# Hybrid encoder layer on one core: the order of four output products and the roles of two accumulator banks

## The chip, the cores and the metric

The kernel runs on one core of one Trainium2 chip. The metric is device time in microseconds (us): the median of three runs was 1156.17 us (1155.99 to 1157.1). Five engines work side by side, each through its own list of instructions in a fixed order: TensorE (PE, matmuls; its weight loads are listed as PEld), VectorE (DVE), ScalarE (ACT), GpSimd (POOL) and SyncE (SP, which here issues the DMAs). They wait for one another through semaphores only.

## The reference

One encoder layer over 4096 tokens of width 1024, in float32:

```
h    = rmsnorm(x) ;  proj = h @ w_in
q, k, v, g_a, u_p, g_p = split(proj)
a    = banded_attention(q, k, v, rel_bias, sink) * silu(g_a)    # 8 query heads, 2 kv heads, window 128
p    = multiscale_pool(u_p) * silu(g_p)                         # windows 2, 4, 8, 16
out  = x + rmsnorm(concat(a, p) @ w_out)
```

Banded attention takes blocks of 128 queries against three blocks of keys, adds a relative bias, appends a sink logit, and normalizes. The last line, the output projection `[a, p] @ w_out` with its norm, is the part whose order is changed.

## The kernel before

Every float32 operand of a matmul is kept as two float16 halves (high and low), so one product takes three matmuls for each slice of the contraction. The program has two halves. The first computes the gate and pooling projections and stores them; it isn't touched by the change. The second half walks over the sequence from its end to its start, in blocks of 128 queries (b = 31 down to 0) and in units of 256 tokens (unit u holds blocks 2u and 2u+1). For each unit it projects k, v and q, runs attention for both blocks, and multiplies the result by `w_out`.

That last multiplication is done with Strassen-Winograd sums: seven products of half size in place of eight. They are called 11, 12, 22, s1, s2, s3, s4 after the operand. Each is 12 matmuls of 128 x 512 (`product`, L1700, matmul L1708) into one PSUM bank. Two of them are added on top of another inside the bank (`acc=True`): 12 on 11, and s4 on s1. The left operands are made from the gated attention output and the pooled branch: ACT casts the high half to float16 (`high`, L1610), POOL subtracts to get the low half (`low`, L1614). Three sums on DVE (`sum1`, `sum3`, `sum2`, L1643 to L1649) and one on POOL (`sum4`) come ahead of the casts of s2, s3, s1 and s4.

What leaves the banks: `begin` (ACT copy, L1728) saves 11 by itself to `mo`, before 12 is added onto it in the same bank. `gain11` (DVE, L1738) and `square` (ACT, L1733) read 11+12 from that bank when it is complete. `add` (DVE, L1749) reads s2, s3, 22, s1 and s1+s4, each from its bank.

PSUM: three banks with the tags acc0, acc1 and acc2 are shared by all of the products, the projections of k, v and q (matmul L1300) and one side of the attention output (`values`, L1545). Four more banks hold scores (L1340), and one the other side of the output. A new use of a bank waits until all readers of the old one are done.

The order is written out by hand. `due(t, fn, ...)` puts a call with a planned time into a list; `pe(us, fn, ...)` does the same for TensorE and advances a planned clock `now`. At the end the list is sorted by planned time (and, where two are equal, by the order in which they were put in), and each engine gets its instructions in that order. An engine takes its instructions strictly in that order, whatever is ready. The steps of the loop (L2022) are, for odd b and u = b//2:

- scores of b, first half; s4 of unit u+2; k and v of unit u-1 into bank 2 (for b = 27 these two change places); `values` of b+1 into bank 0 (bank 1 for b = 27); scores of b, second half; then of unit u+1 the products 22 (bank 2), 11 (bank 0), s2 (bank 1), and 12 (bank 0, on 11).

and for even b:

- scores, first half; first half of q of unit u-1 into bank 1; `values` of b+1 into bank 0; scores, second half; second half of q into bank 1; then of unit u+1 the product s3 into bank 0 and s1 into bank 1.

A softmax (`softmax`, L1421) follows each scores: on DVE four `logits` (L1368), on ACT four `exps` (L1379), on DVE a reciprocal of the sums (`denominators`, L1386 and L1389), on ACT four `probs` (L1401), on DVE four `rests` (L1409), and a transposing DMA. `exps` also reads the sink logits, which POOL copies into the tile (`sinks`, L1351). The planned times that matter below, counted from T, the planned end of `values` in an odd step: cast of s2 T+1.8; the four `exps` T+1.9, T+2.7, T+3.5, T+4.3; `probs` from T+5.6; `rests` from T+6.2; casts of s3, s1 and s4 T+10.7, T+11.3, T+12.0, each with its `low` 0.65 later; the next `sinks` T+12.7. `begin` is planned for 1.0 before the end of product 11, `gain11` for the end of 12, `square` 0.1 after it, the `add` of s2 for the end of s2.

Thirty weight loads of one column (L1715; ten in the first units) are spread through each of 11, 22, s2 and 12; they run beside the matmuls.

Of the kernel before, what the change touches and what calls it, by code (L numbers as in the profile page):

```python
# [13 lines left out]
ALU = mybir.AluOpType  # L14
# [9 lines left out]
NB = S // P  # L24
# [15 lines left out]
O11, O12, O21, O22, OT1, OT2, OT4, OT3 = range(8)  # L40
HK = KT // 2
UT = 2 * P
NU = S // UT
# [95 lines left out]
def hybrid_layer(ctx: ExitStack, tc, io, out):  # L139
    nc = tc.nc  # L140
# [74 lines left out]
    with ExitStack() as actx:  # L215
# [23 lines left out]
        def turn(name):  # L239
            turns[name] += 1  # L240
            return turns[name] % 2
# [386 lines left out]
        def pair(q, op, i, scale, key, group):  # L628
            src, r, w = raws[q][:, i], quarter_keys(q, i), f"w{slot[q, op]}"
            do("ACT", act(D) + 0.1, key, w_high, q, op, src, scale, r=r + [f"sw{group}"],  # L630
               w=[f"{w}h"])
            do("DVE", dve(D) + 0.06, key + 0.1, w_low, q, op, src, scale,
               r=r + [f"sw{group}", f"{w}h"], w=[f"{w}l"])
# [343 lines left out]
        b = turn("n2")  # L977
        for j in range(4):
            ld(9.5 + 0.1 * j, wut[:, j], io["w_uT"][j], 0.5, w=[f"wut{j}"])
            z = turn("sq")  # L980
            for half in range(2):
                t = U0 + 4 * j + 2 * half
# [291 lines left out]
    gpost = pb1.tile([P, D], F32, name="gpost")  # L1274
# [41 lines left out]
    def due(t, fn, *args):  # L1316
        plan.append((t, len(plan), fn, args))
# [103 lines left out]
    def softmax(b, half, t):  # L1421

        for i in range(4):
            due(t + 0.1 + 0.67 * i, logits, b, half, i)
            due(t + 0.8 + 0.8 * i, exps, b, half, i)
            due(t + 4.5 + 0.6 * i, probs, b, half, i)
            due(t + 5.1 + 0.62 * i, rests, b, half, i)
        due(t + 4.3, denominators, b, half)
        due(t + 7.8, turn, b, half)
# [159 lines left out]
    at, yf, y_t, mo_t, z_t, ss_t, xr_t, rs_t = {}, {}, {}, {}, {}, {}, {}, {}  # L1589
# [74 lines left out]
    LO, HI = slice(0, 512), slice(512, D)  # L1664
    last_z = {}

    def last_product(i, name, o, c, first):

        if first:

            n = {(1, 0): 0, (1, 1): 2, (0, 0): 1}.get((i, c))
            last_z[i, c] = (
                gemm.tile([P, 512], F32, name=f"z{i}{c}", tag=f"acc{n}") if n is not None
                else s_t[0][:, 0]
            )
        y = y_t[0, name]
        n = 0
        for k in range(HK):
            for yi, wi in ((0, 0), (0, 1), (1, 0)):
                nc.tensor.matmul(  # L1680
                    last_z[i, c], y[:, k, yi, :], wo[o][:, wi, k, :],
                    start=(first and n == 0), stop=(not first and n == 3 * HK - 1),
                    skip_group_check=True,
                )
                n += 1
# [31 lines left out]
    def open_unit(u):  # L1717
        if u > 1:
            mo_t[u] = [
                pb.tile([P, D], F32, name=f"mo{u}_{i}", tag=f"mo{i}", bufs=2 - i) for i in range(2)  # L1720
            ]
        else:
            mo_t[u] = [spare32("x", 2 * u + i) for i in range(2)]
        ss_t[u] = pb.tile([P, 4], F32, name=f"ss{u}", tag="ss")

    def begin(u):
        open_unit(u)
        nc.scalar.copy(mo_t[u][0][:, HI], z_t[u, 0])  # L1728

    def square(u, i, c, bank=None):  # L1730
        junk = pb.tile([P, 512], BF16, name=f"jkb{u}_{i}{c}", tag="junk", bufs=1)
# [2 lines left out]
            junk, src, AF.Square, scale=2.0**-5, accum_out=ss_t[u][:, 2 * i + c : 2 * i + c + 1]  # L1734
        )

    def gain11(u):
        nc.vector.tensor_tensor(  # L1738
            out=mo_t[u][0][:, LO], in0=z_t[u, 0], in1=gpost[:, LO], op=ALU.mult
        )  # L1740

    def gain(u, i, cs, eng=nc.gpsimd):
# [47 lines left out]
    def pe(us, fn, *args):  # L1790

        due(now[0], fn, *args)
        now[0] += us
        return now[0]
# [4 lines left out]
    def visit(b, half):  # L1799
        now[0] = max(now[0], free[0])  # L1800
        t = max(pe(1.1, scores, b, half), free[1])
        softmax(b, half, t)
        free[:] = t + 2.9, t + 7.9
# [10 lines left out]
    def do_q(u, half, late=0.0, bank=1):  # L1814
        due(pe(5.3, proj_q, u, half, bank) - 1.0 + late, keep_q, u, half)

    def attend(b, bank):
        t = pe(2.0, values, b, bank)
        due(t - 0.3, copy_o, b)
        due(t, gate, b)  # L1820
        if b % 2:
            pair(t + 0.8, b // 2, "11", a11)
        else:
            sums(b // 2, t + 0.7)

    M = 2.6
    SP0 = 10

    def spaces(u):
        return 30 if u < NU - 2 else SP0  # L1830

    def mix_p1(u):
        due(pe(M, product, u, "11", O11, 0, None, spaces(u)) - 1.0, begin, u)

    def mix_p4(u):
        pe(M, product, u, "22", OT4, 2, None, spaces(u))

    def mix_p2(u):
        t = pe(M, product, u, "12", O21, 0, True, spaces(u))
        due(t, gain11, u)  # L1840
        due(t + 0.1, square, u, 0, 0, 0)

    def mix_p6(u):
        due(pe(M, product, u, "s2", OT2, 1, None, spaces(u)), add, u, (0, HI), (0, HI), 1)

    def mix_p7(u):
        t = pe(M, product, u, "s3", OT3, 0)
        due(t - 2.0, add, u, (1, HI), (0, HI), 0)
        due(t - 1.9, add, u, (1, LO), (1, HI), 2)
        due(t + 1.4, square, u, 1, 0)  # L1850
        due(t + 2.0, gain, u, 1, LO)

    def mix_p5(u):
        t = pe(M, product, u, "s1", OT1, 1)
        due(t, add, u, (1, HI), (1, HI), 1)
        due(t + 0.7, square, u, 1, 1)
        due(t + 1.4, gain, u, 1, HI)
        finish(u, 1, t + 4.0)

    def mix_p3(u):  # L1860
        bank = int(u < NU - 1)
        t = pe(M, product, u, "s4", O22, bank, True)
        due(t, add, u, (0, HI), (0, HI), bank)
        due(t + 0.7, square, u, 0, 1)
        due(t + 1.4, gain, u, 0, HI)
        due(t + (5.5 if u == NU - 1 else 4.0), mean, u, 0)
        due(t + 13.1, residual, u, 0, slice(0, D))
        due(t + 14.5, store, u, 0, slice(0, D))
# [11 lines left out]
    def at_(t, fn, *args):  # L1880
        due(z + t, fn, *args)
# [140 lines left out]
    for b in reversed(range(2, NB - 4)):  # L2022
        u = b // 2
        t0 = now[0]
        due(t0 + 10.0, load_ga, b)
        if b % 2 == 0 and b > 2:
            due(t0 + 9.0, load_xr, u + 1, 1)
            due(t0 + 9.0, load_xr, u + 1, 0)
        visit(b, 0)
        if b % 2:  # L2030
            for step in ((do_kv, u - 1), (mix_p3, u + 2))[:: 1 if b == NB - 5 else -1]:
                step[0](step[1])
            attend(b + 1, int(b == NB - 5))
            visit(b, 1)
            mix_p4(u + 1)
            mix_p1(u + 1)
            mix_p6(u + 1)
            mix_p2(u + 1)
        else:
            do_q(u - 1, 0)  # L2040
            attend(b + 1, 0)
            visit(b, 1)
            do_q(u - 1, 1)
            due(now[0] + 2.1, load_x, u - 3)
            if b > 2:
                mix_p7(u + 1)
                mix_p5(u + 1)
        if b % 2:
            due(now[0] - 1.0, pool_in, u, 0)
            due(now[0] + 2.0, pool_in, u, 1)  # L2050
            pair(t0 + 8.1, u + 1, "22", a22)
            pair(t0 + 8.7, u + 1, "12", a12)
# [3 lines left out]
    z = now[0]  # L2056

    at_(0.0, scores, 1, 0)
    at_(1.1, product, 2, "s3", OT3, 0)
    at_(3.7, product, 2, "s1", OT1, 1)  # L2060
    at_(6.3, product, 1, "11", O11, 0)
    at_(8.9, product, 2, "s4", O22, 1, True)
    at_(11.5, values, 2, 2)
    at_(13.6, scores, 1, 1)
    at_(14.7, product, 1, "12", O21, 0, True)
    at_(17.3, product, 1, "22", OT4, 2)
    at_(19.9, scores, 0, 0)
    at_(20.8, product, 1, "s2", OT2, 1)
    at_(23.4, product, 1, "s3", OT3, 0)
    at_(26.0, product, 1, "s1", OT1, 1)  # L2070
    at_(28.6, scores, 0, 1)
    at_(29.5, last_product, 1, "22", O21, 0, True)
    at_(32.1, product, 1, "s4", O22, 1, True)
    at_(34.7, values, 1, None)
    at_(36.8, last_product, 1, "22", O22, 1, True)
    at_(39.4, last_product, 0, "12", O21, 0, True)
# [9 lines left out]
    soft(0, 0, 24.9, 25.6, 29.4, 29.5, 29.7, 31.7)  # L2086
    soft(0, 1, 31.6, 32.3, 34.3, 34.4, 34.5, 36.5)

    at_(3.7, add, 2, (1, HI), (0, HI), 0)
    at_(5.5, add, 2, (1, LO), (1, HI), 2)  # L2090
    at_(6.2, add, 2, (1, HI), (1, HI), 1)
    at_(7.0, square, 2, 1, 0)
    at_(9.9, square, 2, 1, 1)
    at_(11.5, add, 2, (0, HI), (0, HI), 1)
    at_(12.3, square, 2, 0, 1)
    at_(11.1, gain, 2, 1, LO, V)
    at_(11.8, gain, 2, 1, HI, V)
# [3 lines left out]

    cast(5.8, 6.4, 1, "22", a22, G)
    cast(6.4, 10.2, 1, "12", a12, G)
    at_(9.0, begin, 1)
    at_(13.7, gate, 2)
    at_(14.4, sum1, 1)
    at_(15.1, sum3, 1)
# [1 line left out]
    at_(16.55, sum4, 1)  # L2109
    cast(16.6, 18.9, 1, "s2", a11, V)  # L2110
    cast(20.5, 20.55, 1, "s3", a21, G)
    at_(19.1, gain11, 1)
    at_(16.58, square, 1, 0, 0, 0)
    cast(21.7, 21.8, 1, "s1", a_s1, G)
    at_(22.3, add, 1, (0, HI), (0, HI), 1)
    cast(24.8, 25.0, 1, "s4", a12, G)
    at_(27.0, add, 1, (1, HI), (0, HI), 0)
    at_(27.7, add, 1, (1, LO), (1, HI), 2)
    at_(28.5, square, 1, 1, 0)
    at_(28.6, add, 1, (1, HI), (1, HI), 1)  # L2120
    at_(31.2, square, 1, 1, 1)
    at_(35.0, add, 1, (0, HI), (0, HI), 1)
    at_(36.6, square, 1, 0, 1)
    at_(40.7, gain, 1, 1, LO, V)
    at_(41.4, gain, 1, 1, HI, V)
# [110 lines left out]
```

## Time and profile before

| | before |
|---|---|
| median of 3 runs | 1156.17 us (1155.99 to 1157.1) |
| the profiled execution's own time | 1156.7 us |
| its span, first to last instruction | 1154.8 us |
| PE busy | 1141.8 us, 99% of the span |
| DVE busy | 941.0 us, 81% |
| ACT busy | 717.3 us, 62% |
| POOL busy | 313.5 us, 27% |
| granted TensorE clock, mean | 0.995 |

A busy PE isn't a PE at its peak, since the ends of matmuls are modelled; the starts are recorded. In lists of instructions over time, the columns are: start in us from the start of the span, duration in us, engine, line, operation, output<-inputs, shape, and how many were merged into the row (x12); in brackets the idle time of the engine just before it, with what ended it. In groups by wait, the columns are total us, times and the longest.

### The profile page before, as it was taken

How to read it: one execution, taken by the hardware profiler on the slowest of the kernel's cores; microseconds unless marked ns; L12 is line 12 of the kernel's file. 1: busy time of each engine (PE TensorE's matmuls, PEld its weight loads, DVE VectorE, ACT ScalarE, POOL GpSimd, SP SyncE). 2: the span in 40 equal slices, each digit the busy share in tenths (PEclk: the TensorE clock that was granted, in tenths of full speed). 3: DMA queues.
4: the chain of work that ended last, by engine and by line, in shares of the span. 5: the costliest groups of instructions: out<-in, count | busy, mean ns of one | idle time of the engine just before them, and what ended most of it. 6: DMA issues, size and time to landing. Idle time of an engine off the chain costs nothing. (4 is left out here: it accounts for less than half of the span.)

```text
span 1154.8 us, 37344 instructions
## 1 busy us (share of the span) xinstructions
PE 1141.8 (99%) x15196; PEld 898.3 (78%) x16676; DVE 941.0 (81%) x1874; ACT 717.3 (62%) x1485; POOL 313.5 (27%) x309
## 2 busy tenths in 40 slices
PE   8999999999999999999999999999999999999997
PEld 6998888888888888886667677677776767767743
DVE  7989969987898973468788887878888888787886
ACT  7875545646565442266666776676667667667672
POOL 0102121111111110210434433532533443343231
PEclk8999999999999999999999999999999999999999
DMA  9644677776567565299976887787888698778795
GB/s 341 232 138 123 247 230 247 247 260 225 188 207 254 174 165 153 65 279 242 262 179 149 198 216 135 208 197 174 182 200 191 147 198 214 134 205 162 139 253 158
DMA packets 301701, 228.66 MB, mean 198 GB/s; under 512 B 219568, under 2 KB 259504, under 8 KB 296928
## 3 DMA queue, kind: packets, MB, share of 16 engines
q1 hardware_dynamic: 301536, 226.30, 73.9%
q8 instruction: 124, 2.03, 0.7%
q14 instruction: 41, 0.34, 0.1%
HBM read 114.68 MB, written 60.34 MB: 152 GB/s over the span
## 5 line engine op out<-in xcount | busy, mean ns | idle before, releaser
L703 PEld LDWEIGHTS <-wq 128*128 128x128 f16 x4104 | 402.0, 98 | 46.6
L703 PE MATMUL y<-xt,wq 128*128 128x256 f16 x1512 | 175.8, 273 | 0.0
L1300 PE MATMUL aq<-xb,xb 128*128 128x256 f16 x1024 | 173.4, 273 | 0.2 <-DVE q L1290 0.2
L1379 ACT ACTIVATE p<-p,nm 128x385 f32<-128x385 f32 (+1 forms) x256 | 152.8, 598 | 30.5 <-POOL p L1351 19.1
L1300 PEld LDWEIGHTS <-xb 128*128 128x128 f16 x1536 | 150.2, 98 | 26.5 <-issue 8.2
L1708 PE MATMUL ms<-wo,ys 128*128 128x512 f16 x720 | 164.4, 379 | 0.5 <-DVE mo L1749 0.5
L1409 DVE SCALAR_TENSOR_TENSOR pn<-p,rd,pn 128x384 f16<-128x384 f32 (+1 forms) x256 | 154.9, 657 | 6.3 <-ACT pn L1401 6.2
L1368 DVE CUSTOM_DVE_ANT_0 p<-s,nt,nsink 128x384 f32<-128x384 f32 (+1 forms) x256 | 155.9, 665 | 1.7 <-PE s L1340 1.7
L1300 PE MATMUL aq<-xb,xt 128*128 128x256 f16 x512 | 139.6, 273 | 0.0
L1401 ACT ACTIVATE pn<-p,rd 128x384 f16<-128x384 f32 (+1 forms) x256 | 135.0, 596 | 5.6 <-ACT p L1379 2.2
L311 POOL TENSOR_TENSOR yt<-yt,sg 128x512 f32<-128x512 f32 (+2 forms) x32 | 51.1, 1596 | 321.4 <-DVE yt L314 252.3
L1708 PE MATMUL m<-wo,y 128*128 128x512 f16 x540 | 121.8, 379 | 0.0
L1708 PEld LDWEIGHTS <-ys 128*128 128x128 f16 x720 | 68.7, 97 | 66.8 <-issue 3.8
L1300 PE MATMUL kv<-xb,xb 128*128 128x256 f16 x512 | 86.8, 273 | 0.0
L1744 POOL TENSOR_TENSOR mo<-mo,gpost 128x512 f32<-128x512 f32 x39 | 63.8, 1635 | 82.9 <-ACT jkb L1733 81.8
L1300 PEld LDWEIGHTS <-xt 128*128 128x128 f16 x768 | 75.1, 98 | 9.8 <-issue 0.2
L1715 PEld LDWEIGHTS <-y 128*1 128x1 f16 x1110 | 44.9, 83 | 35.4
L1300 PE MATMUL kv<-xb,xt 128*128 128x256 f16 x256 | 69.8, 273 | 0.0
L813 ACT COPY cc<-y 128x512 f32<-128x512 f32 x42 | 24.5, 584 | 69.5 <-PE y L703 57.4
L703 PE MATMUL plain<-xb,wq 128*128 128x256 f16 x576 | 67.3, 276 | 0.0
L1386 DVE TENSOR_SCALAR den<-den 128x4 f32<-128x4 f32 x64 | 11.8, 184 | 64.2 <-ACT p L1379 64.2
L1614 POOL TENSOR_TENSOR ys<-at,ys 128x512 f16<-128x512 f32 x28 | 37.4, 1334 | 89.1 <-ACT ys L1610 54.8
(223 smaller groups left out, 2008.7 us busy)
## 6 DMA issues: line engine op xcount, KB each, us to landing
nt<-in_xT SPq DMA_DIRECT2D x28, 512.0 KB
x_scr<-xb SPq DMA_DIRECT2D x14, 1024.0 KB
xb<-x_scr SPq DMA_DIRECT2D x14, 1024.0 KB
xr<-in_x SPq DMA_DIRECT2D x28, 512.0 KB
out<-xr SPq DMA_DIRECT2D x28, 512.0 KB
xn<-in_x SPq DMA_DIRECT2D x27, 512.0 KB
ga_scr<-cc SPq DMA_DIRECT2D x64, 128.0 KB
raw<-in_w_out SPq DMA_DIRECT2D x16, 512.0 KB
```

The source lines that it names most:

```text
L311: eng.tensor_tensor(out=out, in0=in0, in1=in1, op=op)
L703: nc.tensor.matmul(b[:, s], wq[:, slot[q, op], wv, s, k, :], x[:, xv, k, :], start=(first and k + s + wv + xv == 0), stop=(last and k == H ...
L813: A.copy(dst, bank_t[bk])
L1300: nc.tensor.matmul(acc, w[:, j, k, :], x[:, kh, v, kt, :], start=(n == 0), stop=(n == 3 * KT - 1),)
L1368: nc.vector.tensor_tensor_reduce(out=p_t[b, half][:, hh, :nk], in0=s_t[jj][:, gg, :nk], in1=bias[:, h, lo : lo + nk], scale=negc[:, h : h ...
L1379: nc.scalar.activation(p[:, hh, : nk + 1], p[:, hh, : nk + 1], AF.Exp, bias=nm_t[b, half][:, hh : hh + 1], scale=-1.0, accum_out=den_t[b, ...
L1401: nc.scalar.activation(prob_view(b, half)[:, 0, i], p_t[b, half][:, i, :nk], AF.Copy, scale=rd_t[b, half][:, i : i + 1],)
L1409: nc.vector.scalar_tensor_tensor(out=pn4[:, 1, i], in0=p_t[b, half][:, i, :nk], scalar=rd_t[b, half][:, i : i + 1], in1=pn4[:, 0, i], op0= ...
L1614: eng.tensor_tensor(out=y[:, :, 1], in0=f(u), in1=y[:, :, 0], op=ALU.subtract)
L1708: nc.tensor.matmul(z_t[u, tag], y[:, k, yi, :], wo[o][:, wi, k, :], start=(n == 0 and acc is None), stop=(n == 3 * HK - 1), skip_group_che ...
L1715: nc.tensor.ldweights(y[:, k, yi, :1])
L1744: eng.tensor_tensor(out=mo, in0=mo, in1=gpost[:, cs], op=ALU.mult)
```

## The change

In the loop, the four products of an odd step come in the order 11, 22, 12, s2 instead of 22, 11, s2, 12. Banks 0 and 1 change roles in what follows, in the loop and in the written-out end: `values` goes to bank 1, both halves of q to bank 0, s3 to bank 1, s1 and s4 to bank 0. 11 and 12 stay in bank 0 and s2 in bank 1 in the loop; in the written-out end for units 2, 1 and 0 all of bank 0 and bank 1 are exchanged. No instruction is added or removed, and no operand's size is changed. The planned times are computed from the order, so `begin`, `gain11`, `square` and the `add` of s2 get other planned times too.

```diff
@@ last_product
-            n = {(1, 0): 0, (1, 1): 2, (0, 0): 1}.get((i, c))
+            n = {(1, 0): 1, (1, 1): 2, (0, 0): 0}.get((i, c))
@@
-    def begin(u):
+    def begin(u, bank=0):
         open_unit(u)
-        nc.scalar.copy(mo_t[u][0][:, HI], z_t[u, 0])
+        nc.scalar.copy(mo_t[u][0][:, HI], z_t[u, bank])
@@
-    def gain11(u):
+    def gain11(u, bank=0):
         nc.vector.tensor_tensor(
-            out=mo_t[u][0][:, LO], in0=z_t[u, 0], in1=gpost[:, LO], op=ALU.mult
+            out=mo_t[u][0][:, LO], in0=z_t[u, bank], in1=gpost[:, LO], op=ALU.mult
         )
@@
     def mix_p7(u):
-        t = pe(M, product, u, "s3", OT3, 0)
-        due(t - 2.0, add, u, (1, HI), (0, HI), 0)
+        t = pe(M, product, u, "s3", OT3, 1)
+        due(t - 2.0, add, u, (1, HI), (0, HI), 1)
...
     def mix_p5(u):
-        t = pe(M, product, u, "s1", OT1, 1)
-        due(t, add, u, (1, HI), (1, HI), 1)
+        t = pe(M, product, u, "s1", OT1, 0)
+        due(t, add, u, (1, HI), (1, HI), 0)
...
     def mix_p3(u):
-        bank = int(u < NU - 1)
-        t = pe(M, product, u, "s4", O22, bank, True)
-        due(t, add, u, (0, HI), (0, HI), bank)
+        t = pe(M, product, u, "s4", O22, 0, True)
+        due(t, add, u, (0, HI), (0, HI), 0)
@@ the loop
-            attend(b + 1, int(b == NB - 5))
+            attend(b + 1, 1)
             visit(b, 1)
+            mix_p1(u + 1)
             mix_p4(u + 1)
-            mix_p1(u + 1)
+            mix_p2(u + 1)
             mix_p6(u + 1)
-            mix_p2(u + 1)
         else:
-            do_q(u - 1, 0)
-            attend(b + 1, 0)
+            do_q(u - 1, 0, bank=0)
+            attend(b + 1, 1)
             visit(b, 1)
-            do_q(u - 1, 1)
+            do_q(u - 1, 1, bank=0)
@@ the written-out end: 0 and 1 exchanged in every product, add, begin, gain11 and square
-    at_(6.3, product, 1, "11", O11, 0)
+    at_(6.3, product, 1, "11", O11, 1)
...
-    at_(9.0, begin, 1)
+    at_(9.0, begin, 1, 1)
...
```

In the loop, `mix_p1` is product 11, `mix_p4` 22, `mix_p2` 12 and `mix_p6` s2.

More of the change, by code (lines that the diff above doesn't have):

```diff
@@ L2058, in hybrid_layer @@
     at_(0.0, scores, 1, 0)
-    at_(1.1, product, 2, "s3", OT3, 0)
-    at_(3.7, product, 2, "s1", OT1, 1)
-    at_(6.3, product, 1, "11", O11, 0)
-    at_(8.9, product, 2, "s4", O22, 1, True)
+    at_(1.1, product, 2, "s3", OT3, 1)
+    at_(3.7, product, 2, "s1", OT1, 0)
+    at_(6.3, product, 1, "11", O11, 1)
+    at_(8.9, product, 2, "s4", O22, 0, True)
     at_(11.5, values, 2, 2)
     at_(13.6, scores, 1, 1)
-    at_(14.7, product, 1, "12", O21, 0, True)
+    at_(14.7, product, 1, "12", O21, 1, True)
     at_(17.3, product, 1, "22", OT4, 2)
     at_(19.9, scores, 0, 0)
-    at_(20.8, product, 1, "s2", OT2, 1)
-    at_(23.4, product, 1, "s3", OT3, 0)
-    at_(26.0, product, 1, "s1", OT1, 1)
+    at_(20.8, product, 1, "s2", OT2, 0)
+    at_(23.4, product, 1, "s3", OT3, 1)
+    at_(26.0, product, 1, "s1", OT1, 0)
     at_(28.6, scores, 0, 1)
     at_(29.5, last_product, 1, "22", O21, 0, True)
-    at_(32.1, product, 1, "s4", O22, 1, True)
+    at_(32.1, product, 1, "s4", O22, 0, True)
     at_(34.7, values, 1, None)
@@ L2087, in hybrid_layer @@
     soft(0, 1, 31.6, 32.3, 34.3, 34.4, 34.5, 36.5)
-    at_(3.7, add, 2, (1, HI), (0, HI), 0)
+    at_(3.7, add, 2, (1, HI), (0, HI), 1)
     at_(5.5, add, 2, (1, LO), (1, HI), 2)
-    at_(6.2, add, 2, (1, HI), (1, HI), 1)
+    at_(6.2, add, 2, (1, HI), (1, HI), 0)
     at_(7.0, square, 2, 1, 0)
     at_(9.9, square, 2, 1, 1)
-    at_(11.5, add, 2, (0, HI), (0, HI), 1)
+    at_(11.5, add, 2, (0, HI), (0, HI), 0)
     at_(12.3, square, 2, 0, 1)
@@ L2111, in hybrid_layer @@
     cast(20.5, 20.55, 1, "s3", a21, G)
-    at_(19.1, gain11, 1)
-    at_(16.58, square, 1, 0, 0, 0)
+    at_(19.1, gain11, 1, 1)
+    at_(16.58, square, 1, 0, 0, 1)
     cast(21.7, 21.8, 1, "s1", a_s1, G)
-    at_(22.3, add, 1, (0, HI), (0, HI), 1)
+    at_(22.3, add, 1, (0, HI), (0, HI), 0)
     cast(24.8, 25.0, 1, "s4", a12, G)
-    at_(27.0, add, 1, (1, HI), (0, HI), 0)
+    at_(27.0, add, 1, (1, HI), (0, HI), 1)
     at_(27.7, add, 1, (1, LO), (1, HI), 2)
     at_(28.5, square, 1, 1, 0)
-    at_(28.6, add, 1, (1, HI), (1, HI), 1)
+    at_(28.6, add, 1, (1, HI), (1, HI), 0)
     at_(31.2, square, 1, 1, 1)
-    at_(35.0, add, 1, (0, HI), (0, HI), 1)
+    at_(35.0, add, 1, (0, HI), (0, HI), 0)
     at_(36.6, square, 1, 0, 1)
```

## The prediction

> **What bounds the kernel now.** I read the page first, then the PE's rows of one unit in the second half, then the other engines' rows of the same stretch, and last the groups of waits.
>
> ```profile
> span 1154.8 us, 37344 instructions
> ...
> PE 1141.8 (99%) x15196; PEld 898.3 (78%) x16676; DVE 941.0 (81%) x1874; ACT 717.3 (62%) x1485; POOL 313.5 (27%) x309
> ...
> PEclk8999999999999999999999999999999999999999
> ```
>
> PE is busy for 99% of the span at a full clock, so a change moves the time only by making PE stop, or by taking away a stop that it has. The PE rows of the unit with its second scores at 860.17:
>
> ```profile
> 850.55 0.60 PE L1708 MATMUL ms<-wo,ys 128*128 128x512 f16 x2
> ...
> 860.17 0.96 PE L1340 MATMUL s<-k_all,q 64*32 64x288 f16 x48
> 861.06 5.35 PE L1708 MATMUL m<-wo,y 128*128 128x512 f16 x24
> 866.25 2.88 PE L1708 MATMUL ms<-wo,ys 128*128 128x512 f16 x12
> 868.97 0.38 PE L1708 MATMUL m<-wo,y 128*128 128x512 f16 x1
> ...
> 871.65 0.93 PE L1340 MATMUL s<-k_all,q 64*32 64x288 f16 x48
> 872.51 0.28 PE L1300 MATMUL aq<-xb,xb 128*128 128x256 f16 x1
> ...
> 891.82 0.60 PE L1708 MATMUL ms<-wo,ys 128*128 128x512 f16 x2
> ```
>
> They are s4, scores, 22 and 11 together, s2, the start of 12, the next scores, the first q, and s4 of the next unit. One unit takes 891.82 - 850.55 = 41.27 us, with nothing between the products: 22 and 11 take 5.19, or 2.60 each. Only s2 is longer, 868.97 - 866.25 = 2.72, and a group of the waits says why; the row under it is the view of `begin`'s line:
>
> ```profile
> PEld L1708 <- POOL ys L1614: 2.7, 12, 0.2
> ```
>
> ```profile
> L1728 ACT COPY mo<-m x14: 560/564/586, 531.7 to 1074.3; 128x512 f32<-128x512 f32 x14
> ```
>
> In 12 units the third matmul of s2 waits for POOL's low half; the cost to PE is 2.72 - 2.60 = 0.12. `begin` counts the units: the first two of the 14 are 15 (written out) and 14; the other 12, units 13 to 2, follow each other at 41.27.
>
> ACT in the same stretch (s2 cast, three of four `exps`, `begin`, first `probs`, casts of s3 and s1, `square`, cast of s4, next `exps`), then DVE (reciprocal of the sums, residual, `rests`, `add` of s2, `gain11`) and POOL (low half of s2, s3, s1, s4, and `sinks`):
>
> ```profile
> 864.88 0.62 ACT L1610 CAST ys<-at 128x512 f16<-128x512 f32 x1 [3.75 <-DVE at L1649]
> 865.54 0.62 ACT L1379 ACTIVATE p<-p,nm 128x385 f32<-128x385 f32 x1
> ...
> 866.16 0.60 ACT L1379 ACTIVATE p<-p,nm 128x385 f32<-128x385 f32 x1
> ...
> 866.76 0.60 ACT L1379 ACTIVATE p<-p,nm 128x385 f32<-128x385 f32 x1
> ...
> 867.95 0.56 ACT L1728 COPY mo<-m 128x512 f32<-128x512 f32 x1
> 868.55 2.13 ACT L1401 ACTIVATE pn<-p,rd 128x384 f16<-128x384 f32 x4
> 870.59 0.60 ACT L1610 CAST ys<-at 128x512 f16<-128x512 f32 x1
> 871.85 0.62 ACT L1610 CAST ys<-s 128x512 f16<-128x512 f32 x1 [0.66 <-PE m L1708]
> 873.04 0.60 ACT L1733 ACTIVATE jkb<-m 128x512 bf16<-128x512 f32 x1 [0.57 <-DVE mo L1738]
> 873.53 0.19 ACT L1733 ACTIVATION_READ_ACCUMULATOR jkb<-m 128x1 f32 x1
> 873.62 0.61 ACT L1610 CAST ys<-yf 128x512 f16<-128x512 f32 x1
> 875.63 0.62 ACT L1379 ACTIVATE p<-p,nm 128x385 f32<-128x385 f32 x1 [1.40 <-POOL p L1351]
> ```
>
> ```profile
> 868.08 0.17 DVE L1386 TENSOR_SCALAR den<-den 128x4 f32<-128x4 f32 x1 [0.83 <-ACT p L1379]
> ...
> 868.40 1.28 DVE L1771 SCALAR_TENSOR_TENSOR xr<-mo,rs,xr 128x1024 f32<-128x1024 f32 x1
> 869.61 2.20 DVE L1409 SCALAR_TENSOR_TENSOR pn<-p,rd,pn 128x384 f16<-128x384 f32 x4
> 871.72 0.68 DVE L1749 TENSOR_TENSOR mo<-ms,mo 128x512 f32<-128x512 f32 x1
> 872.32 0.68 DVE L1738 TENSOR_TENSOR mo<-m,gpost 128x512 f32<-128x512 f32 x1
> ```
>
> ```profile
> 865.58 1.16 POOL L1614 TENSOR_TENSOR ys<-at,ys 128x512 f16<-128x512 f32 x1 [2.86 <-PE m L1708]
> ...
> 871.26 1.57 POOL L1614 TENSOR_TENSOR ys<-at,ys 128x512 f16<-128x512 f32 x1 [3.29 <-ACT ys L1610]
> 872.79 1.16 POOL L1614 TENSOR_TENSOR ys<-s,ys 128x512 f16<-128x512 f32 x1
> 874.31 1.16 POOL L1614 TENSOR_TENSOR ys<-yf,ys 128x512 f16<-128x512 f32 x1 [0.36 <-ACT ys L1610]
> 875.41 0.32 POOL L1351 COPY p<-nsink 128x4 f32<-128x4 f32 x2
> ```
>
> Two rows matter most. `square` waited 0.57 for `gain11`, though it uses nothing that `gain11` makes: both read the bank of 11+12, and the second reader waits for the first. And the next `exps` (875.63) had waited 1.40 for `sinks`, which stand on POOL behind the three low halves.
>
> **The change part by part.** Times are on the clock of this unit, with 860.17 held fixed.
>
> (a) s2 goes last. Its low half ends at 866.74, s2 then starts after 12; the stop of 0.12 goes, in 12 units.
>
> (b) `begin`. Planned for T+5.3 before, it is now planned for T+1.1+2.6-1.0 = T+2.7. That is behind the cast of s2 (T+1.8) and the first `exps`, and level with the second `exps` (T+2.7 too). Adding the plan's numbers in floating point, the tie falls `begin` ahead of the second `exps` in units 13, 12 and 11 and behind it in 14 and 10 to 2. ACT waits for DVE's sums until 864.88, so `begin` starts at 866.76 (866.16 in the three) and takes 0.56. 12 must wait for it. Without a wait 12 would start at 866.25, the old place of s2. With the 0.07 from ACT's end to PE's start (as between ACT's cast, 870.59 + 0.60, and POOL's start, 871.26) it starts at 867.39 or 866.79, 1.14 or 0.54 late. Before, `begin` had ended at 868.51 and 12 started at 868.97: a cover of 0.46, gone.
>
> (c) Behind `begin` on ACT stand `exps` 3 and 4 (in the three units also 2), 0.59 later each (867.95 to 868.55). DVE's reciprocal, the residual and `rests` are a chain without gaps behind them, so DVE comes free at 871.72 + 0.59 = 872.31.
>
> (d) `gain11` and `square` move up, since 12 ends earlier. `gain11` takes DVE's slot at 872.31, ends at 873.00; `square` starts at 873.03. But on ACT `square` (T+9.0) now stands ahead of the casts of s3, s1 and s4 (T+10.7 on), and holds them up while it waits. The cast of s3 goes from 870.59 to 873.03 + 0.59 = 873.62.
>
> (e) The banks. The first q now takes bank 0, after `gain11` and `square`, where it took bank 1 after the `add` of s2. `square`'s sum is out 0.69 after its start (873.04 to 873.53 + 0.19), so with 0.06 to PE's start q begins at about 873.78, not 872.51: 1.27 late, in all units, whether (b) costs 0.54 or 1.14. All other exchanges put a use behind one as old as before: 0 and 1 are swapped in both. 22 and 11 find their banks free for longer.
>
> (f) POOL. The low half of s3 starts 0.69 after its cast (as 873.62 to 874.31 for s4), at 874.31, and s1 and s4 follow at 1.10 each (874.31 to 875.41). For s3 I take 1.16, not 1.57, since it no longer runs beside `add` and `gain11`. So `sinks` starts at 874.31 + 3.30 = 877.61 and the `exps` 0.22 later, at 877.83, not 875.63: 2.20 late.
>
> (g) From these `exps` a chain runs over ACT and DVE through the first q's low half, `rests`, the gate, the next softmax and the three `add`s to s4 of the unit. How long it is when nothing else holds it up is seen in unit 14, where PE did wait for it:
>
> ```profile
> 587.11 0.62 ACT L1379 ACTIVATE p<-p,nm 128x385 f32<-128x385 f32 x1 [1.41 <-POOL p L1351]
> 602.91 0.59 PE L1708 MATMUL ms<-wo,ys 128*128 128x512 f16 x2 [0.47 <-DVE mo L1749]
> ```
>
> 15.80 us. In the steady unit it is 891.82 - 875.63 = 16.19, so the chain has 0.39 to spare. Late by 2.20, it brings s4 at 877.83 + 15.80 = 893.63, 1.81 late. PE's stops at 12, at q and at s4 are not added: each is counted from the old time, and the last, 1.81, holds the others. From s4 to the next 860.17 PE works 9.62 as before, so the unit takes 41.27 + 1.81 = 43.08.
>
> The sum. Units 13 to 3, 11 periods at 1.81: 19.9. Unit 14 already waits on this chain; its reciprocal is held up by something else for longer than (c), and I take 0.2. Unit 2 runs into the written-out end:
>
> ```profile
> 1066.50 0.96 PE L1340 MATMUL s<-k_all,q 64*32 64x288 f16 x48
> 1081.97 0.62 ACT L1379 ACTIVATE p<-p,nm 128x385 f32<-128x385 f32 x1 [1.40 <-POOL p L1351]
> 1100.84 0.59 PE L1708 MATMUL ms<-wo,ys 128*128 128x512 f16 x2
> ```
>
> There s4 comes 18.87 after the `exps`, with DVE busy nearly all the way; 2.20 less a cover of about 0.6 (11 of unit 1 stands between) gives 1.6. Together 19.9 + 0.2 + 1.6 = 21.7 on the profiled 1156.7, or 1178.4. That execution lies 0.5 above the median, so I predict 1178 for the median.
>
> Bounds. If the low half of s3 keeps its 1.57, each unit takes 0.41 more: 1182.5. If the chain had 0.9 to spare, q's 1.27 would be the last stop: 12 x 1.27 + 0.4 = 15.6, 1172.
>
> **The rivals.**
>
> 1. Only `begin` counts. The casts recover behind `square` because POOL and ACT have idle time later. Then nine units cost 1.14 - 0.12, three 0.54 - 0.12, and unit 14 about 0.2: 10.7, 1167. For it: POOL is busy 27%. Against it: the 15.80 above is measured with PE waiting.
>
> 2. q's bank is the last stop: 1172, above. For it: 0.39 is a small difference of two rows.
>
> 3. Not slower. If ACT's order came out with `begin` before the cast of s2, in the 3.75 that ACT sits idle, and `square` behind the casts, 12 would find its bank free and only (a) would be left: 12 x 0.12 = 1.4 saved, 1154.7. It decides whether `begin` ends before 866.2. The planned times are 0.9 against it, and `square` is 1.7 ahead of the casts; ACT's rows stand in planned order throughout. So the exchange would have to mean something else than the plan says.
>
> 4. The clock. The page shows it full in every slice but the first, with a PE that hardly stops; no row has it with PE stopping three times in a unit. If it halved for the length of one product, 2.60, in each of 12 units, 31 would come on top: 1209. Against it: no stop forecast here is over 1.3. The Trainium skill (TensorE: Matmul & The Clock Gate, Part 1) has the array fall to half its rate after an idle window of about 3.4 us; by that rule, too, nothing falls here.
>
> **How the numbers follow.** Forecast, 1178: 0.58; its own bounds are 1174 (a chain with 0.7 to spare) and 1183. Rival 1: 0.12. Rival 2: 0.14. Rival 3: 0.06, of which 0.02 over the bound for faster. Rival 4: 0.02. The rest, 0.08, is later stops that I don't see, up to 1190. The range 1166 to 1186 takes in the forecast, rivals 1 and 2 and part of the rest. A measurement of this kernel tells 0.2% (2.3 us) from no change; slower by that 0.94, within 0.04, faster 0.02.
>
> **What would show it.** Right: 12's first matmul waits for `begin` in each unit; s2 takes 2.60 to 2.70 without a wait for POOL; the casts of s3, s1, s4 stand behind `square`, which waits for `gain11`; the first `exps` of an even step come 17.7 after the second scores of the odd one; s4 waits for DVE's `add`; units are 43.1 apart, PE's share falls to about 97%. Wrong: (b) if 12 starts on time; (d) and (f) if `exps` come at 15.5 still; (g) if q waits and s4 doesn't. Equal units at 41.3 would refute all of it.

## The result and the profile after

The changed kernel takes 1177.08 us (median of 4 runs, 1176.74 to 1177.65); the kernel before, timed beside it, 1156.08 (median of 4, 1155.51 to 1157.1). The ratio is 1.0183, with a 95% interval of 1.017 to 1.0196: 21 us slower. Among the runs below, one of square_late (6770.44 us) and three of the kernel before (1314.4 to 6770.48 us) were slow, and they are left out of every median and range.

The page of the kernel after, its span, its engines and the granted clock:

```profile
span 1175.1 us, 37331 instructions
...
PE 1142.6 (97%) x15196; PEld 899.3 (77%) x16676; DVE 938.2 (80%) x1874; ACT 716.1 (61%) x1485; POOL 308.2 (26%) x309
...
PEclk9999999999999999999999999999999999999999
```

No engine has noticeably more to do: PE is busy for 1142.6 us against 1141.8, over a span that is 20.3 longer. The clock is full in every slice. So the time went into stops of PE. The waits of PE in the second half (us in total, times, longest):

```profile
PE m L1708 <- ACT mo L1728: 10.3, 13, 1.0
PE ms L1708 <- DVE mo L1749: 5.6, 12, 0.5
PE aq L1300 <- ACT jkb L1733: 2.4, 4, 0.7
```

PE stops at 12 for `begin` (L1728), at s4 for the `add`s (L1749), and in four units it shows a stop at q for `square` (L1733). None of the three is among the waits of before, apart from one 0.5 at s4 in unit 14. Their total, 18.3, is near the loss. Where each comes from is seen in the unit that answers to the one of the prediction, PE first (second scores, 11 and 22, 12, s2, next scores, first q, s4 of the next unit):

```profile
869.66 0.96 PE L1340 MATMUL s<-k_all,q 64*32 64x288 f16 x48
870.55 5.35 PE L1708 MATMUL m<-wo,y 128*128 128x512 f16 x24
876.87 2.75 PE L1708 MATMUL m<-wo,y 128*128 128x512 f16 x12 [0.96 <-ACT mo L1728]
879.45 2.75 PE L1708 MATMUL ms<-wo,ys 128*128 128x512 f16 x12
882.13 0.93 PE L1340 MATMUL s<-k_all,q 64*32 64x288 f16 x48
883.16 0.27 PE L1300 MATMUL aq<-xb,xb 128*128 128x256 f16 x1
...
903.05 0.81 PE L1708 MATMUL ms<-wo,ys 128*128 128x512 f16 x3 [0.46 <-DVE mo L1749]
```

ACT, DVE and POOL in the same stretch:

```profile
874.38 0.62 ACT L1610 CAST ys<-at 128x512 f16<-128x512 f32 x1 [3.77 <-DVE at L1649]
875.04 0.62 ACT L1379 ACTIVATE p<-p,nm 128x385 f32<-128x385 f32 x1
...
875.65 0.60 ACT L1379 ACTIVATE p<-p,nm 128x385 f32<-128x385 f32 x1
...
876.25 0.56 ACT L1728 COPY mo<-m 128x512 f32<-128x512 f32 x1
...
882.42 0.60 ACT L1733 ACTIVATE jkb<-m 128x512 bf16<-128x512 f32 x1 [1.76 <-DVE mo L1738]
...
883.00 0.61 ACT L1610 CAST ys<-at 128x512 f16<-128x512 f32 x1
...
887.25 0.62 ACT L1379 ACTIVATE p<-p,nm 128x385 f32<-128x385 f32 x1 [2.60 <-POOL p L1351]
```

```profile
879.58 2.20 DVE L1409 SCALAR_TENSOR_TENSOR pn<-p,rd,pn 128x384 f16<-128x384 f32 x4
881.70 0.68 DVE L1738 TENSOR_TENSOR mo<-m,gpost 128x512 f32<-128x512 f32 x1
882.30 0.68 DVE L1749 TENSOR_TENSOR mo<-ms,mo 128x512 f32<-128x512 f32 x1
```

```profile
883.69 1.17 POOL L1614 TENSOR_TENSOR ys<-at,ys 128x512 f16<-128x512 f32 x1 [6.22 <-ACT ys L1610]
884.80 1.17 POOL L1614 TENSOR_TENSOR ys<-s,ys 128x512 f16<-128x512 f32 x1
885.92 1.16 POOL L1614 TENSOR_TENSOR ys<-yf,ys 128x512 f16<-128x512 f32 x1
887.02 0.32 POOL L1351 COPY p<-nsink 128x4 f32<-128x4 f32 x2
```

Read from the top: `begin` starts after the second `exps`, when 12 should already have begun; `square` stands ahead of the casts and waits 1.76 for `gain11`; the cast of s3 starts only at 883.00, so POOL's three low halves and `sinks` behind them are late, and the next `exps` wait 2.60 for `sinks`. Distances from the unit's second scores, typical of units 10 to 3 (differences of the rounded rows can be 0.01 off); the last row is the period of the loop:

| from second scores to | before | predicted | after |
|---|---|---|---|
| start of 12 | 6.08, were it not for s2 | 7.22 | 7.21 |
| first q | 12.35 | 13.61 | 13.49 |
| next `exps` | 15.47 | 17.66 | 17.58 |
| s4 | 31.65 | 33.46 | 33.39 |
| second scores of the next unit | 41.27 | 43.08 | 43.00 |

The next unit's scores close the account of the loop. The second scores of unit 13 and of unit 2, in the kernel after:

```profile
611.70 0.96 PE L1340 MATMUL s<-k_all,q 64*32 64x288 f16 x48
...
1084.63 0.84 PE L1340 MATMUL s<-k_all,q 64*32 64x288 f16 x40
```

Between them lie 472.93, against 1066.50 - 612.52 = 453.98 before: 18.95 more in 11 periods, or 1.72 each. From unit 2 to the end of the span it takes 1175.10 - 1084.63 = 90.47 against 1154.84 - 1066.50 = 88.34: 2.13 more. Ahead of unit 13 the profile of after is 0.82 shorter: unit 14 begins 1.56 sooner (568.90 for 570.46) and takes 42.80 for 42.06. Nearly all of the 1.56 lies between the second scores of unit 15 and those of unit 14 (40.99 for 42.44), where PE waits twice for a DMA in the profile of before; the section on the hardware comes back to it. 18.95 + 2.13 - 0.82 = 20.3, the difference of the spans.

### The profile page after: what moved, and what is told of

Read it like the earlier page. It is cut to its first block, busy times and chain, and to the rows that moved or that the text cites. A ratio compares the mean times of both kernels' runs of the same rounds, so it can differ in the third digit from the quotient of the medians.

```text
span 1175.1 us, 37331 instructions
## 1 busy us (share of the span) xinstructions
PE 1142.6 (97%) x15196; PEld 899.3 (77%) x16676; DVE 938.2 (80%) x1874; ACT 716.1 (61%) x1485; POOL 308.2 (26%) x309
## 5 line engine op out<-in xcount | busy, mean ns | idle before, releaser
L1708 PE MATMUL m<-wo,y 128*128 128x512 f16 x540 | 121.7, 379 | 11.0 <-ACT mo L1728 10.3
L1614 POOL TENSOR_TENSOR ys<-at,ys 128x512 f16<-128x512 f32 x28 | 32.6, 1163 | 126.3 <-ACT ys L1610 126.3
```

The lines of the kernel that those rows point to most:

```text
L1614: eng.tensor_tensor(out=y[:, :, 1], in0=f(u), in1=y[:, :, 0], op=ALU.subtract)
L1708: nc.tensor.matmul(z_t[u, tag], y[:, k, yi, :], wo[o][:, wi, k, :], start=(n == 0 and acc is None), stop=(n == 3 * HK - 1), skip_group_che ...
```

## The experiments

Every kernel here computes the whole output. The ratios are to the kernel before, timed on the same chip beside them (its median lay between 1156.0 and 1156.73).

### The copy ahead of the cast of s2 (begin_early)

On the changed kernel:

```diff
-        due(pe(M, product, u, "11", O11, 0, None, spaces(u)) - 1.0, begin, u)
+        due(pe(M, product, u, "11", O11, 0, None, spaces(u)) - 2.0, begin, u)
```

> The changed kernel, with the copy `begin` planned 2.0 instead of 1.0 ahead of the end of product 11 (T+1.7), so that it stands ahead of the cast of s2 on ACT. My theory (PE is late by the last of three releases: 12 by `begin`, q by `square`, s4 by the chain behind the casts): 12 starts on time and the `exps` are no longer 0.59 late, but `square` still holds up the casts, so the `exps` of the even step come 17.1 after the odd step's second scores, s4 waits, a unit takes 42.5 and the kernel about 1171 us. Rival that only the wait for `begin` counts: units of 41.2 to 41.3, 1155 to 1157 us. Rival that q's bank is the last release: q starts 0.65 late, units of 41.9, about 1164 us.

1171.55 us (1171.28 to 1174.16), ratio 1.0137 (1.0122 to 1.0152). 12 is on time and the next scores come 11.36 after the second scores. The rest of the chain stays, only shorter: q 13.01, `exps` 17.10, s4 32.91, period 42.52. From `exps` to s4 it is 15.81, as in after (15.80). PE's waits:

```profile
PE aq L1300 <- ACT jkb L1733: 10.0, 13, 1.0
PE ms L1708 <- DVE mo L1749: 5.6, 12, 0.5
```

So 12's being 1.12 late is worth only 0.48 a unit: most of it was time that PE would have spent at q and at s4 anyway. That the stops are not to be added is shown; and `begin` is not the main cause.

### `square` behind the three casts (square_late)

On the changed kernel:

```diff
-        due(t + 0.1, square, u, 0, 0, 0)
+        due(t + 3.4, square, u, 0, 0, 0)
```

> The changed kernel, with `square` of 11+12 planned 3.4 instead of 0.1 after the end of 12 (T+12.3), so that it stands behind the casts of s3, s1 and s4 on ACT. `begin` stays where the change puts it. My theory: the casts are no longer held up, the `exps` of the even step come at about 15.6, the chain releases s4 in time, and what is left is q, which still waits for `square` and starts 1.16 late; a unit takes 42.4, the kernel about 1170 us. Rival that only `begin` counts: no change against the changed kernel, 43.0 and 1177 us. If the casts weren't what holds up the `exps`, s4 would still wait and the unit stay at 43.0.

1168.34 us (median of 3, 1168.33 to 1169.05), ratio 1.0106 (1.0089 to 1.0123). The next `exps` come at 15.54, as before the change (15.47), though 12 still starts 1.12 late, and the wait at s4 is gone from the list:

```profile
PE m L1708 <- ACT mo L1728: 10.1, 13, 1.0
PE aq L1300 <- ACT jkb L1733: 2.4, 4, 0.7
```

The period is 42.41: q starts at 13.50, 1.15 later than before, and nothing behind it makes that longer (41.27 + 1.15 = 42.42). This is the world of rival 2, with q's bank as the last stop.

### `sinks` ahead of the low halves (sinks_early)

In the changed kernel `sinks` of an even step's first softmax are planned at the start of that step, ahead of the three low halves on POOL, and nothing else is moved:

```diff
         else:
+            due(t0 - 0.3, sinks, b, 0)
             do_q(u - 1, 0, bank=0)
```

> The changed kernel, with the `sinks` of the even step's first softmax planned at T+11.2, ahead of the low halves of s3, s1 and s4 on POOL, instead of behind them. Nothing else is moved: `begin`, `square` and the casts stay where the change puts them. My theory: the `exps` follow the cast of s4 on ACT, at about 14.9 after the odd step's second scores instead of 17.6, so s4 is released in time and q, 1.16 late, is the last; a unit takes 42.4 and the kernel about 1169 us, as with `square` behind the casts. If the `exps` weren't held by `sinks` but by the casts themselves, no change: 43.0 and 1177 us.

1168.98 us (1168.44 to 1169.12), ratio 1.0112 (1.0096 to 1.0128), period 42.40. ACT and POOL of this kernel:

```profile
878.73 0.60 ACT L1733 ACTIVATE jkb<-m 128x512 bf16<-128x512 f32 x1 [1.76 <-DVE mo L1738]
879.32 0.61 ACT L1610 CAST ys<-at 128x512 f16<-128x512 f32 x1
...
880.86 0.62 ACT L1379 ACTIVATE p<-p,nm 128x385 f32<-128x385 f32 x1
```

```profile
873.73 0.19 POOL L1351 COPY p<-nsink 128x4 f32<-128x4 f32 x1
880.00 1.16 POOL L1614 TENSOR_TENSOR ys<-at,ys 128x512 f16<-128x512 f32 x1 [6.09 <-ACT ys L1610]
```

`square` still waits its 1.76, and the casts and low halves are as late as in after. Only this one copy is out of the way: `exps` follow the last cast with no wait, and the wait at s4 is gone (PE's list has 12's 10.3 and q's 2.3 alone). So what carried the lateness of the casts to s4 was `sinks` behind the low halves on POOL, not the low halves themselves. This and the run before are two cuts through one chain, and both leave the same 42.40.

### The banks alone (banks_alone)

The changed kernel with the four products in their old order 22, 11, s2, 12:

```diff
-            mix_p1(u + 1)
             mix_p4(u + 1)
-            mix_p2(u + 1)
+            mix_p1(u + 1)
             mix_p6(u + 1)
+            mix_p2(u + 1)
```

> The exchange of the banks alone: the changed kernel with the four products back in the order 22, 11, s2, 12. My theory: `begin` and the casts are where they were, 12 doesn't wait, the `exps` come at 15.5, but q in bank 0 waits for `gain11` and `square`, which end 1.2 after the old release, so q starts 1.27 late and nothing after it makes it later; a unit takes 42.5, and unit 14, where `gain11` stands behind the residual, costs 1.6 more: about 1173 us. Rival that only `begin` counts: 1156 us, no change against the kernel before. Rival that a swap of two banks is neutral: the same.

1173.58 us (1173.35 to 1173.92), ratio 1.015 (1.0135 to 1.0165). `exps` come at 15.47 and s2 has its old stop of 0.12 back; the period is 42.52, all from one place:

```profile
PE aq L1300 <- ACT jkb L1733: 17.4, 13, 3.1
```

With the old order 12 ends last, so q waits for `gain11` and `square` of a product that has only just ended: it starts at 13.61 for 12.35, 1.26 late in each of 12 units, and waits 3.1 in unit 14. In the changed kernel 12 starts 1.60 sooner (7.21 for 8.81), and the same wait shows in four units only.

### The order alone (order_alone)

The kernel before with only the four lines of the order changed, on the old banks:

```diff
             visit(b, 1)
+            mix_p1(u + 1)
             mix_p4(u + 1)
-            mix_p1(u + 1)
+            mix_p2(u + 1)
             mix_p6(u + 1)
-            mix_p2(u + 1)
```

> The order 11, 22, 12, s2 alone, in the kernel before with its old banks. My theory: 11 now follows `values` in the same bank and waits some 0.9 for the gate's read of it; 12 then waits for `begin` until the same moment as in the changed kernel, 7.2 after the second scores, so the 0.9 costs nothing; q in bank 1 waits for the `add` of s2, which now stands behind `gain11`, and starts 1.15 late; the `exps` come at 17.6 and s4 is again the last release: a unit takes 43.0 and the kernel about 1177 us, as much as both parts together. Rival that the parts add up: the changed kernel's 21 less what the banks alone cost, 1160 to 1165 us. Rival that `values` in the same bank adds its 0.9: 1187 us.

1177.31 us (1176.76 to 1178.69), ratio 1.018 (1.0163 to 1.0197): the same as with the banks. Most periods are 43.00 (`exps` 17.58, s4 33.39), as in after; one of 43.76 and one of 43.23 stand between them. In the first of these PE also waits 0.57 for a transposing DMA (L1545, at 741.55); what makes up the rest, and the second, stays open. PE's main waits:

```profile
PE m L1708 <- DVE at L1583: 10.0, 12, 0.9
PE ms L1708 <- DVE mo L1749: 5.1, 11, 0.5
```

11 now comes straight behind the scores and needs bank 0, which `values` has just used: it waits 0.8 to 0.9 for DVE to read that out. 12 then waits only 0.2 for `begin`. The two stops, one behind the other, bring PE to the same point. So the exchange of the banks did do something: it took away the wait of 11. It gained nothing, because `begin` held 12 to the same time.

### The new order with the chain mended (order_mended)

On the kernel before: the new order; only `values` of the odd steps into bank 1; `begin` 1.0 earlier; the `add` of s2 ahead of `gain11`; and `square` behind the casts.

```diff
-        due(pe(M, product, u, "11", O11, 0, None, spaces(u)) - 1.0, begin, u)
+        due(pe(M, product, u, "11", O11, 0, None, spaces(u)) - 2.0, begin, u)
...
-        due(t, gain11, u)
-        due(t + 0.1, square, u, 0, 0, 0)
+        due(t + 2.6, gain11, u)
+        due(t + 3.4, square, u, 0, 0, 0)
...
-        due(pe(M, product, u, "s2", OT2, 1, None, spaces(u)), add, u, (0, HI), (0, HI), 1)
+        due(pe(M, product, u, "s2", OT2, 1, None, spaces(u)) - 0.1, add, u, (0, HI), (0, HI), 1)
...
-            attend(b + 1, int(b == NB - 5))
+            attend(b + 1, 1)
```

> The new order 11, 22, 12, s2 in the kernel before, with what my theory says it needs: `values` of the odd step in bank 1 (11 then finds bank 0 free), `begin` at T+1.7, the `add` of s2 ahead of `gain11` (T+11.4 and T+11.5), `square` behind the casts (T+12.3); the first q, s3, s1 and s4 stay in their old banks. My theory: no release is late; s2 no longer waits for POOL, but q is then released by the `add` of s2 at the old time, so a unit takes 41.2 and the kernel 1155 to 1156 us, no difference from before. Rival that the order costs something of itself that I haven't named: over 1160 us.

1157.38 us (median of 11, 1155.43 to 1159.03), ratio 1.0012 (1.0003 to 1.0021). The period is 41.20, 0.07 below before. Nearly all of the 21 us is back; what is left over is of the size of the loss at unit 14, which takes 45.23 against 42.06 before (86.22 against 84.50 from unit 15's second scores to unit 13's). PE and DVE there:

```profile
582.84 0.27 PE L1300 MATMUL aq<-xb,xb 128*128 128x256 f16 x1 [2.40 <-DVE mo L1749]
```

```profile
580.00 2.19 DVE L1771 SCALAR_TENSOR_TENSOR xr<-mo,rs,xr 128x1024 f32<-128x1024 f32 x1
582.11 0.68 DVE L1749 TENSOR_TENSOR mo<-ms,mo 128x512 f32<-128x512 f32 x1
```

There the residual of unit 15 stands on DVE ahead of the `add` of s2, for which q waits, and takes 2.19, for 1.28 in the loop before. I had expected 1155 to 1156 and missed this.

### What s2's stop is worth (s2_low_last)

The kernel before, in the old order. In s2 the eight matmuls that take the high half go first and the four that take POOL's low half last; only the order of the sum changes.

```diff
-        for k in range(HK):
-            for yi, wi in ((0, 0), (0, 1), (1, 0)):
+        terms = [(k, yi, wi) for k in range(HK) for yi, wi in ((0, 0), (0, 1), (1, 0))]
+        if name == "s2":
+            terms.sort(key=lambda s: s[1])
+        if True:
+            for k, yi, wi in terms:
```

> The kernel before, old order and old banks; in product s2 alone the eight matmuls with the high half of the left operand come first and the four with its low half last, so that none waits for POOL's low half. It gives the price of the stop that the change takes away in s2. My prediction's term (a) says 0.12 a unit, 1.4 us, so 1154.8 us. But q's bank is released by the `add` of s2, whose place on DVE doesn't move, some 0.05 ahead of q: if that holds, only 0.05 to 0.08 a unit is left, 1155.3 us or no difference.

1155.11 us (median of 11, 1154.45 to 1157.28), ratio 0.9997 (0.9988 to 1.0006): no difference that can be told. In the profile s2 has no stop, but the period falls only by 0.07, to 41.20. The next scores and the first q show where the rest goes:

```profile
872.39 0.93 PE L1340 MATMUL s<-k_all,q 64*32 64x288 f16 x48
873.34 0.27 PE L1300 MATMUL aq<-xb,xb 128*128 128x256 f16 x1
```

0.95 lie between them, where they were 0.86 before (871.65 to 872.51): q waits for the `add` of s2, which DVE's chain doesn't bring sooner.

### The same with DVE's chain shorter (s2_low_last_res_late)

The run before, and the residual and its store 5.7 later, behind `gain11` on DVE:

```diff
-        due(t + 13.1, residual, u, 0, slice(0, D))
-        due(t + 14.5, store, u, 0, slice(0, D))
+        late = 5.7 * (u < NU - 1)
+        due(t + 13.1 + late, residual, u, 0, slice(0, D))
+        due(t + 14.5 + late, store, u, 0, slice(0, D))
```

> As the one before it, and the residual of the unit in hand (DVE, 1.28 long) planned 5.7 later, behind `gain11`, with its store, so that `rests` and the `add` of s2 end earlier and q's bank is free in time. My theory: the whole 0.12 a unit is gained, 1154.8 us, 0.12% under the kernel before, if nothing behind the residual's new place is late by more than the 0.39 that the chain has to spare; the next `logits` start up to 1.2 later, which the `exps` can bear, since they wait 1.4 for `sinks`. If they can't, the kernel is slower than before.

1154.71 us (median of 11, 1153.57 to 1155.98), ratio 0.999 (0.9981 to 0.9999). The period is 41.14, and q comes 12.22 after the second scores, 0.86 after the next ones: now the whole 0.13 of s2's stop is gone.

### Both lessons in the old order (old_order_best)

The run before, and `sinks` of the even steps early as above:

```diff
+            due(t0 - 0.3, sinks, b, 0)
             do_q(u - 1, 0)
```

> The kernel before with three things: in s2 the matmuls with the low half last, the residual and its store 5.7 later, and `sinks` of the even step's first softmax ahead of the three low halves on POOL. My theory: units of 41.13 as in the run without `sinks` moved, since PE is then the only bound; the `exps` come at about 14.7; unit 14, where s4 waits for the chain, is 0.8 shorter. About 1154 us, 0.2% under the kernel before. If the chain isn't what unit 14 waits for, 1154.7 as in the run before it.

1152.42 us (median of 7, 1152.09 to 1154.92), ratio 0.9972 (0.9961 to 0.9982). In the loop the period is 41.14 as in the run before. Unit 14 falls from 42.58 to 41.46: the chain from `exps` to s4, on which PE waited there, starts sooner. The stretch from unit 2's second scores to the end falls from 88.34 to 87.91. These two, 1.1 and 0.4, are the 1.5 by which the spans of the two profiles differ (1153.2 and 1151.7); the medians lie 2.3 apart, and no profile shows the other 0.8. In the whole second half the list has one wait of PE for another engine left, 0.3 at q.

### Both lessons in the new order (order_mended_2)

`order_mended` with the residual late in every unit, unit 15 too, and `sinks` early:

```diff
+        late = 5.7 if u < NU - 1 else 1.5
+        due(t + 13.1 + late, residual, u, 0, slice(0, D))
+        due(t + 14.5 + late, store, u, 0, slice(0, D))
...
+            due(t0 - 0.3, sinks, b, 0)
```

> The new order, mended as in the first such run, with the residual behind `gain11` in every unit (in unit 15's too, where it stood ahead of the `add` of s2 and made q of the next step 2.3 late) and `sinks` of the even step ahead of the low halves. My theory: units of 41.13, no late q in unit 14: about 1154 us, the same as the best of the old order, so the order of the four products is worth nothing by itself in either direction. If the new order has a cost of its own that I haven't named, it stays at 1156 us or over.

1152.88 us (median of 10, 1151.8 to 1155.77), ratio 0.9976 (0.9966 to 0.9985), period 41.14, unit 14 41.45. One unit of it, second scores, 11, 22 and 12 in one row, s2:

```profile
857.05 0.96 PE L1340 MATMUL s<-k_all,q 64*32 64x288 f16 x48
857.94 7.94 PE L1708 MATMUL m<-wo,y 128*128 128x512 f16 x36
865.72 2.75 PE L1708 MATMUL ms<-wo,ys 128*128 128x512 f16 x12
```

36 matmuls of the three products run without a stop. Both orders come to the same period and, by their intervals, the same time; they beat the kernel before by 0.28% and 0.24%. The order of the products itself is worth nothing that can be told, either way, once what hangs on it is put right (in the old order that takes in the other order of s2's sum).

## Why the prediction was right

The forecast of 1178 stands against 1177.08. Its mechanism held step by step: the stop of s2 and the end were mis-sized, a few terms were off by 0.1, and one price had a wrong reason behind it.

(a) The stop of s2: mis-sized. After the change s2 runs without a wait, as said. But the 0.12 was priced as a saving of its own. In s2_low_last only 0.07 of it came through, since q then waits for the `add` of s2. In the changed kernel it was worth nothing at all, because s4 sets the period. It didn't enter the forecast, only the rivals.

(b) `begin`: right. It starts behind the second `exps` in units 10 to 2 and ahead of it in 13, 12 and 11, and 12 starts 1.12 and 0.52 late, for 1.14 and 0.54. The tie in the plan fell as worked out. That this stop isn't the one that counts is shown by begin_early, which takes it away and gets back 5.5 of the 21 us.

(c), (d) Right. `exps` 3 and 4 come behind the copy, DVE comes free at 12.04 after the second scores (881.70 - 869.66; predicted 12.14), and `square` waits 1.76 on ACT with the casts behind it. The PSUM page of the Trainium skill (PSUM — Partial Sum Buffer, Terms) has two engines on one bank and quadrant at once as an error, two reads included; by that rule the two readers have to be kept apart, and the trace shows that they are: `square` starts 0.04 after `gain11` ends (881.70 + 0.68 = 882.38 to 882.42), though it uses nothing of it. Putting `square` behind the casts brings `exps` back to 15.54.

(e) q's bank: 1.14 late for 1.27. 0.10 of it is DVE's earlier end in (c). With the wait at s4 cut away (square_late, sinks_early), this term sets the period at 42.40: units 13 to 11, where 12 is only 0.52 late, are as long as the others.

(f) `sinks`: 2.11 late for 2.20, again the 0.10. The choice of 1.16 and not 1.57 for the low half of s3 was right (883.69: 1.17), but the reason given for it was not: the 0.41 comes from the last of `rests`, in which this low half starts before the change, and not from `add` and `gain11` (see the section on the hardware). It now starts behind all three, so both reasons lead to the same price, and that was luck. sinks_early shows the place: with the three low halves just as late, the loss at s4 goes.

(g) The chain of 15.80: exact. In after it is 903.05 - 887.25 = 15.80, and 15.81 with the copy early. With the 0.39 to spare that was read from two rows, 2.11 late gives 1.72, and the period grew by 1.73. That a chain length taken from one unit (14), where PE waited on it, held in units 13 to 3 is what settled the case against rivals 1 and 2.

The sum. 11 x 1.72 = 18.95 for 19.9, 0.9 less. The end was put at 1.6 and took 2.13, 0.5 more. The step that failed there is the cover of about 0.6 that I gave to 11 of unit 1. Before, 11 and s4 of the end come 16.28 and 18.87 after unit 2's `exps`; after the change too:

```profile
1102.22 0.62 ACT L1379 ACTIVATE p<-p,nm 128x385 f32<-128x385 f32 x1 [2.60 <-POOL p L1351]
```

```profile
1118.50 2.75 PE L1708 MATMUL m<-wo,y 128*128 128x512 f16 x12 [0.71 <-DVE mo L1749]
1121.09 2.75 PE L1708 MATMUL ms<-wo,ys 128*128 128x512 f16 x12
```

11 waits for an `add` of the same DVE chain, so it covered nothing: these `exps` are 2.12 late, and so is all behind them. Unit 14 was put at 0.2. It takes 42.80 for 42.06, but the profile of before has two waits for a DMA ahead of it, which fall into this comparison. From unit 15's second scores to unit 13's it is 83.79 after; in s2_low_last, the old order without those waits, it is 83.63. The difference of 0.16 is near the 0.2, though one profile of each can't show it. The errors of -0.9 and +0.5 have opposite signs; that they partly cancel is luck, though both are small beside the 21.

The rivals. 1 (only `begin`) fell, since begin_early leaves 15 of the 21. 2 (q's bank last) is what the kernel becomes when either link behind the casts is cut; its price of 1172 was too high by 3 to 4, of which 12 x 0.13 = 1.6 is q, 1.14 late and not 1.27. 3 (not slower) was refuted for the kernel as changed. Its two conditions, `begin` ahead of the cast of s2 and `square` behind the casts, are both in order_mended, at 1157.38; but that kernel also keeps q, s3, s1 and s4 in their old banks and has the `add` of s2 ahead of `gain11`. By themselves the two would not have been enough, as far as the rows go: with `begin` early the first q of the changed kernel still starts at 13.01, 0.66 late, since it takes the bank that `gain11` and `square` read. The two alone were not run. 4 (the clock) did not occur: stops of up to 1.0, up to three times in a unit, leave every slice of the clock at 9, and so does the stop of 3.1 in unit 14 of banks_alone. The Trainium skill (TensorE: Matmul & The Clock Gate, Part 1) has the array fall to half its rate after an idle window of about 3.4 us; the trace agrees, so far as it has stops.

What I had not seen is that the parts are not additive: the banks alone cost 16.9 by the medians (1173.58 against 1156.73 beside it), the order alone 20.6, both together 21.0. Each holds PE at a point through which the other's loss would pass too.

## What to carry to other kernels

Where engines take their work strictly in a written order, price a moved instruction by what stands behind it on each queue it is in, follow that until something waits for data and not for its turn, and take the last stop rather than the sum. The slack of a chain can be read off where it is visible: one unit in which the bound engine did wait for it gives its length, and the steady unit gives the spare. When a loss has run through such a chain, cutting any one link ends it, and often the cheapest is a small instruction that stands behind work it doesn't need (here one copy of 128 x 4, 0.19 us long).

## What the runs showed of the hardware

Work on POOL and work on DVE can hold each other up. The low half of s3 (POOL, 128 x 512 to float16) takes 1.53 to 1.57 in the loop of the kernel before, where it starts about 0.54 before the end of `rests` on DVE, and 1.16 or 1.17 in the kernel after, where it starts behind them. `add` and `gain11`, beside which it also runs before the change, do not cost it anything: in order_mended_2 it runs beside both and takes 1.17. DVE (`rests`, `add`, `gain11`, `residual`) and POOL (low halves of s3, s1, s4) of that kernel:

```profile
866.08 2.21 DVE L1409 SCALAR_TENSOR_TENSOR pn<-p,rd,pn 128x384 f16<-128x384 f32 x4 [0.73 <-ACT pn L1401]
868.51 0.69 DVE L1749 TENSOR_TENSOR mo<-ms,mo 128x512 f32<-128x512 f32 x1 [0.23 <-PE ms L1708]
869.12 0.68 DVE L1738 TENSOR_TENSOR mo<-m,gpost 128x512 f32<-128x512 f32 x1
869.72 1.80 DVE L1771 SCALAR_TENSOR_TENSOR xr<-mo,rs,xr 128x1024 f32<-128x1024 f32 x1
```

```profile
868.15 1.17 POOL L1614 TENSOR_TENSOR ys<-at,ys 128x512 f16<-128x512 f32 x1 [3.15 <-ACT ys L1610]
869.27 1.16 POOL L1614 TENSOR_TENSOR ys<-s,ys 128x512 f16<-128x512 f32 x1
870.39 2.15 POOL L1614 TENSOR_TENSOR ys<-yf,ys 128x512 f16<-128x512 f32 x1
```

Here `residual` starts while the low half of s1 has 0.71 still to run, and takes 1.80 where it took 1.28 in the loop before; the low half of s4 starts while `residual` has 1.13 to run, and takes 2.15 for 1.16. In each of these cases the one that starts second is longer, by 0.14 to 0.19 less than the first had still to run: 0.41 for 0.55 (871.26 to 871.81 before), 0.52 for 0.71, 0.99 for 1.13. `rests` and `residual` take both of their large inputs from SBUF, the memory of the core's tiles; `add`, `gain11` and `logits` take one from a PSUM bank, and in units 13 to 3 of all the profiles no low half that runs beside these alone takes more than 1.17. That the place of the inputs is what decides is an inference; it was not tried by itself.

The other is that a stretch which no edit touches isn't equally long from profile to profile. Up to the second scores of unit 14 the engines have the same work in the same order in order_alone as in the kernel before; from unit 15's second scores to unit 14's it takes 41.51, the kernel before 42.44, and eight of the twelve profiles 40.99. In the kernel before, PE waits there for a transposing DMA, 0.67 at 546.52 and 0.40 at 569.21, that is in time in the profile of the kernel after. Why it differs stays open.
